# Layer norm with residual: loads of 16 rows instead of 8, and the store queued between the x and the residual load

## The chip, the cores and the metric

One core of a Trainium2 chip. The metric is the device time of one execution in microseconds (us), lower is better. The profile's span is about 1.3 us shorter than that time (237.9 against 239.2 us before).

## The reference

```python
# x, residual: (16, 1024, 512) float32; gamma, beta: (512,)
z = x + residual
mean = np.mean(z, axis=-1, keepdims=True)
var = np.var(z, axis=-1, keepdims=True)
return gamma * (z - mean) / np.sqrt(var + eps) + beta
```

16384 rows of 512 numbers are spread over 128 partitions, 128 rows for each. Below, **"a row" is one row on each of the 128 partitions**: 2 KB per partition, 256 KB in all. So 8 rows are 2 MB and 16 rows 4 MB; x, residual and the result are 128 rows each, 100.67 MB in all.

## The kernel before

The stages: SyncE (SP) issues all large transfers on one queue; GpSimd (POOL) adds the residual to x in place in `zbuf`, 8 rows at a time; ScalarE (ACT) makes the mean and the sum of squares of 4 rows at a time; VectorE (DVE) normalises those 4 rows in place; SP stores them. `zbuf` is a ring of 64 rows, `rbuf` one of 32.

```python
X_CHUNKS = [8] * 15 + [4, 4]          # rows of each load of x
R_CHUNKS = [8] * 15 + [4, 4]          # ... of the residual
OUT_CHUNKS = [16] * 7 + [8, 4, 4]     # rows of each store
Z_ROWS = 64
R_ROWS = 32
STORE_LAG = 40
ADD = 8
# ... cut ...
    stored = 0
    for c, (lo, n) in enumerate(loads_x):             # all on SP, in this order
        asked = lo + n
        while stored < asked - Z_ROWS:                # the ring: x may overwrite
            o = next(i for i, b in enumerate(stores) if b[0] == stored)
            nc.sync.wait_ge(so[o], 16)                # ... only what has been stored
            stored += stores[o][1]
        move(part(zbuf, Z_ROWS, lo, n), dram(xf, lo, n), sx[c])
        while todo_r and todo_r[0][1][0] + todo_r[0][1][1] <= asked:
            rc, (rlo, rn) = todo_r.pop(0)
            wait_rows(s_add, "add", rlo + rn - R_ROWS)
            move(part(rbuf, R_ROWS, rlo, rn), dram(rf, rlo, rn), sr[rc])
        while todo_o and (
            todo_o[0][1][0] + todo_o[0][1][1] <= asked - STORE_LAG or asked == total
        ):
            oc, (olo, on) = todo_o.pop(0)
            wait_rows(s_out, "out", olo + on)         # DVE has written these rows
            move(dram(of, olo, on), part(zbuf, Z_ROWS, olo, on), so[oc])
# ... cut ...
    for c, (lo, n) in enumerate(loads_x):             # POOL
        nc.gpsimd.wait_ge(sx[c], 16)
        for rc, (rlo, rn) in enumerate(loads_r):
            if lo <= rlo < lo + n:
                nc.gpsimd.wait_ge(sr[rc], 16)         # the whole residual load
                for a in range(rlo, rlo + rn, ADD):
                    # zbuf rows a..a+8 += rbuf rows, then s_add += 8
# ... cut: ACT and DVE, loops over 4 rows at a time that wait for s_add and for each other
```

Of the kernel before, what the change touches and what calls it, by code (L numbers as in the profile page):

```python
# [10 lines left out]
ALU = mybir.AluOpType  # L11


X_CHUNKS = [8] * 15 + [4, 4]
R_CHUNKS = [8] * 15 + [4, 4]
OUT_CHUNKS = [16] * 7 + [8, 4, 4]

Z_ROWS = 64
R_ROWS = 32
STORE_LAG = 40  # L20


ADD = 8
# [11 lines left out]
def kernel(  # L35
# [13 lines left out]
    of = out.flatten_outer_dims()  # L49
    N, D = xf.shape  # L50
    inv_d = 1.0 / float(D)
    total = N // P
# [5 lines left out]
    def spans(sizes):  # L58
        assert sum(sizes) == total
        return [(sum(sizes[:c]), n) for c, n in enumerate(sizes)]  # L60

    blocks = spans(OUT_CHUNKS)

    def dram(t, lo, n):

        b0, bn = next(b for b in blocks if b[0] <= lo and lo + n <= b[0] + b[1])
        v = t[P * b0 : P * (b0 + bn), :].rearrange("(p j) d -> p j d", p=P)
        return v[:, lo - b0 : lo - b0 + n, :].rearrange("p a b -> p (a b)")

    zbuf = nc.alloc_sbuf_tensor("zbuf", [P, Z_ROWS * D], FP32)  # L70
# [18 lines left out]
    def sem(name):  # L89
        s = nc.alloc_semaphore(name)  # L90
        sems.append(s)
        return s

    loads_x, loads_r, stores = spans(X_CHUNKS), spans(R_CHUNKS), blocks
    sx = [sem(f"sx{c}") for c in range(len(loads_x))]
# [8 lines left out]
    s_out = sem("out")  # L104
    so = [sem(f"so{c}") for c in range(len(stores))]
# [3 lines left out]
    def part(buf, size, lo, n):  # L109
        assert lo % size + n <= size  # L110
        return buf[:, (lo % size) * D : (lo % size + n) * D]
# [16 lines left out]
    todo_r, todo_o = list(enumerate(loads_r)), list(enumerate(stores))  # L128
# [3 lines left out]
    def wait_rows(s, key, rows):  # L132
        if rows > seen[key]:
            nc.sync.wait_ge(s, rows)
            seen[key] = rows

    def move(out, in_, s):
        i = nc.sync.dma_start(out=out, in_=in_).then_inc(s, 16)  # L138
        if len(first) < EARLY:
            first.append(i.ins)  # L140

    stored = 0
    for c, (lo, n) in enumerate(loads_x):
        asked = lo + n
        while stored < asked - Z_ROWS:
            o = next(i for i, b in enumerate(stores) if b[0] == stored)
            assert all(o != t[0] for t in todo_o)
            nc.sync.wait_ge(so[o], 16)
            stored += stores[o][1]
        move(part(zbuf, Z_ROWS, lo, n), dram(xf, lo, n), sx[c])  # L150
        while todo_r and todo_r[0][1][0] + todo_r[0][1][1] <= asked:
            rc, (rlo, rn) = todo_r.pop(0)
            wait_rows(s_add, "add", rlo + rn - R_ROWS)
            move(part(rbuf, R_ROWS, rlo, rn), dram(rf, rlo, rn), sr[rc])
        while todo_o and (
            todo_o[0][1][0] + todo_o[0][1][1] <= asked - STORE_LAG or asked == total
        ):
            oc, (olo, on) = todo_o.pop(0)
            wait_rows(s_out, "out", olo + on)
            move(dram(of, olo, on), part(zbuf, Z_ROWS, olo, on), so[oc])  # L160



    for o, (lo, n) in enumerate(stores[:-1]):
# [7 lines left out]
    for c, (lo, n) in enumerate(loads_x):  # L172
# [3 lines that stand above are left out]
                assert rlo + rn <= lo + n  # L176
                nc.gpsimd.wait_ge(sr[rc], 16)
                for a in range(rlo, rlo + rn, ADD):
# [3 lines left out]
                        out=z, in0=z, in1=part(rbuf, R_ROWS, a, an), op=ALU.add  # L182
# [9 lines left out]
    with act.Fori(0, total // LAP) as lap:  # L192
        z0 = act.snap((lap * (LAP * D)) % (Z_ROWS * D))
        r0 = act.snap(lap * LAP)
        for j in range(SETS):
# [4 lines left out]
            for k in range(TURN):  # L200
                i = act.activation(  # L201
                    out=junk_m[k][:, :],
# [7 lines left out]
            for k in range(TURN):  # L210
                i = act.activation(  # L211
                    out=junk_s[k][:, :],
# [8 lines left out]
                out=std[j][:, :],  # L221
# [9 lines left out]
    with dve.Fori(0, total // LAP) as lap:  # L231
        z0 = dve.snap((lap * (LAP * D)) % (Z_ROWS * D))
        r0 = dve.snap(lap * LAP)
        for j in range(SETS):
# [3 lines left out]
            for k in range(TURN):  # L238
                dve.scalar_tensor_tensor(  # L239
                    out=zk[k],  # L240
# [9 lines left out]
            for k in range(TURN):  # L250
                i = dve.scalar_tensor_tensor(  # L251
                    out=zk[k],
# [53 lines left out]
```

## Time and profile before

| | before |
|---|---|
| time, median | 239.19 us (239.16 to 239.43, 4 runs) |
| span of the profiled execution | 237.9 us |
| busy share DVE / ACT / POOL | 74% / 78% / 60% |
| share of the 16 DMA engines' span used by the queue | 99.3% |

First, lines of the page: the span; the busy share of the DMA engines in 40 equal slices (9 is 90% or more) and the GB/s of each slice; the row of the queue table (packets, MB, share of the 16 engines' span); and two groups of instructions (busy us, mean ns of one, then the idle time before them and what ended it).

```profile
span 237.9 us, 1484 instructions
...
DMA  8999999999999999999999999999999999999996
GB/s 309 441 433 421 433 433 433 419 427 441 421 438 419 438 427 424 468 441 386 427 433 435 441 413 433 430 449 430 413 430 419 457 441 383 455 435 430 421 417 287
...
q1 hardware_dynamic: 6336, 100.67, 99.3%
...
L181 POOL TENSOR_TENSOR zbuf<-zbuf,rbuf 128x4096 f32<-128x4096 f32 (+1 forms) x17 | 142.0, 8353 | 70.6 <-DMA rbuf<-in_residual_dram 70.6
...
L201 ACT ACTIVATE junk_m<-zbuf 128x512 f32 x128 | 74.8, 585 | 31.5 <-POOL zbuf L181 29.1
```

The queue of transfers is never empty from the first slice to the last, at 423 GB/s over the span. The Trainium skill ("HBM Reference", section Specifications) says that a core streaming alone measures about 425 GB/s; this trace agrees. So POOL's 70.6 us of waiting for the residual and ACT's 29.1 us of waiting for POOL cost nothing: the transfers are the limit.

Adds on POOL in order of time (start us, us, engine, line, operation, then the idle time before it and its releaser):

```profile
149.63 8.87 POOL L181 TENSOR_TENSOR zbuf<-zbuf,rbuf 128x4096 f32<-128x4096 f32 x1 [10.78 <-DMA rbuf<-in_residual_dram]
159.40 8.84 POOL L181 TENSOR_TENSOR zbuf<-zbuf,rbuf 128x4096 f32<-128x4096 f32 x1 [0.90 <-DMA rbuf<-in_residual_dram]
179.00 8.86 POOL L181 TENSOR_TENSOR zbuf<-zbuf,rbuf 128x4096 f32<-128x4096 f32 x1 [10.75 <-DMA rbuf<-in_residual_dram]
188.77 8.85 POOL L181 TENSOR_TENSOR zbuf<-zbuf,rbuf 128x4096 f32<-128x4096 f32 x1 [0.91 <-DMA rbuf<-in_residual_dram]
203.56 4.53 POOL L181 TENSOR_TENSOR zbuf<-zbuf,rbuf 128x2048 f32<-128x2048 f32 x1 [5.94 <-DMA rbuf<-in_residual_dram]
```

Where ACT takes up the rows that are added at 179.00 (rows 104 to 112; 24 rows remain then):

```profile
188.08 0.60 ACT L201 ACTIVATE junk_m<-zbuf 128x512 f32 x1 [5.63 <-POOL zbuf L181]
```

DVE's last piece, same columns:

```profile
226.35 2.72 DVE L251 SCALAR_TENSOR_TENSOR zbuf<-zbuf,rstd,beta_p 128x512 f32 x4
```

And the last 38 us in stretches: start and end, its length, then busy us (and instructions) of PE, PEld, DVE, ACT, POOL, then the granted clock, the DMA share and GB/s. A packet is counted in the stretch in which it starts, so a share can come out a little above 1.

```profile
200.00:210.00 10.00, 0.00 (x0) 0.00 (x0) 9.33 (x17) 9.80 (x30) 6.04 (x2) 1.00 1.04 438
210.00:220.00 10.00, 0.00 (x0) 0.00 (x0) 9.14 (x16) 9.59 (x29) 3.02 (x1) 1.00 1.02 439
220.00:230.00 10.00, 0.00 (x0) 0.00 (x0) 8.78 (x15) 3.63 (x11) 0.00 (x0) 1.00 0.97 415
230.00:238.00 8.00, 0.00 (x0) 0.00 (x0) 0.00 (x0) 0.00 (x0) 0.00 (x0) 1.00 0.75 317
```

DVE is done at 226.35 + 2.72 = 229.07 us, and the span ends at 237.9. Until 230 us the DMA share is at least 0.97: the last stores stand in a queue that is still full, so compute is ahead of the transfers by a few us only.

### The profile page before, as it was taken

The page shows a single profiled execution, that of the slowest core. Times are in us where ns is not written, and L with a number is a line of the kernel's source. Part 1 is how long each engine was busy: PE and PEld are TensorE (multiplying, and loading weights), DVE is VectorE, ACT ScalarE, POOL GpSimd, SP SyncE. Part 2 cuts the span into 40 slices and gives each one's busy share as a digit, 9 for nine tenths or more (in the row PEclk, how much of TensorE's full clock was granted, in tenths as well). Part 3 has the DMA queues.
Part 4 walks back from the last instruction along what each step waited for, and adds up shares of the span by engine and source line. Part 5 has one row for each costly group of instructions (what it writes and reads, how often), then busy time and mean ns, then how long its engine had stood idle before and what let it go on. Part 6 is the DMA issues. An engine that isn't in the chain of part 4 may idle for free.

```text
span 237.9 us, 1484 instructions
## 1 busy us (share of the span) xinstructions
PE 3.7 (2%) x4; PEld 1.2 (0%) x4; DVE 177.2 (74%) x290; ACT 185.5 (78%) x545; POOL 142.2 (60%) x21
## 2 busy tenths in 40 slices
PE   0600000000000000000000000000000000000000
PEld 0100000000000000000000000000000000000000
DVE  0000498989898989898989898963989549898950
ACT  2003999999999999999999999739996399999600
POOL 0098988989889407893078930889209892770000
DMA  8999999999999999999999999999999999999996
GB/s 309 441 433 421 433 433 433 419 427 441 421 438 419 438 427 424 468 441 386 427 433 435 441 413 433 430 449 430 413 430 419 457 441 383 455 435 430 421 417 287
DMA packets 6341, 100.68 MB, mean 423 GB/s; under 512 B 706, under 2 KB 706, under 8 KB 708
## 3 DMA queue, kind: packets, MB, share of 16 engines
q1 hardware_dynamic: 6336, 100.67, 99.3%
q14 instruction: 1, 0.01, 0.0%
q10 hardware_dynamic: 4, 0.00, 0.0%
HBM read 67.11 MB, written 33.55 MB: 423 GB/s over the span
## 4 chain that ended last, share of the span: by engine, by line
DMA 49%; ACT 24%; POOL 11%; DVE 5%; issue 4%; SPq 1%; ACTq 1%; DVEq 0%; POOLq 0%
DMA rbuf<-in_residual_dram 36%; ACT junk_s L211 14%; DMA out_dram<-zbuf 13%; POOL zbuf L181 11%; ACT junk_m L201 10%; DVE zbuf L239 3%; DVE zbuf L251 3%; SPq L138 1%; ACTq L201 1%; DVEq L239 0%; ACT std L220 0%; DVE rstd L248 0%; ACTq L192 0%; ACTq L198 0%; DVEq L231 0%
## 5 line engine op out<-in xcount | busy, mean ns | idle before, releaser
L181 POOL TENSOR_TENSOR zbuf<-zbuf,rbuf 128x4096 f32<-128x4096 f32 (+1 forms) x17 | 142.0, 8353 | 70.6 <-DMA rbuf<-in_residual_dram 70.6
L239 DVE SCALAR_TENSOR_TENSOR zbuf<-zbuf,nm,gamma_p 128x512 f32 x128 | 87.1, 742 | 48.7 <-ACT junk_s L211 48.7
L201 ACT ACTIVATE junk_m<-zbuf 128x512 f32 x128 | 74.8, 585 | 31.5 <-POOL zbuf L181 29.1
L211 ACT ACTIVATE junk_s<-zbuf,nm 128x512 f32 x128 | 88.9, 695 | 1.0
L251 DVE SCALAR_TENSOR_TENSOR zbuf<-zbuf,rstd,beta_p 128x512 f32 x128 | 87.1, 743 | 1.1
L211 ACT ACTIVATION_READ_ACCUMULATOR junk_s<-zbuf,nm 128x1 f32 x128 | 23.9, 187 | 0.0
L201 ACT ACTIVATION_READ_ACCUMULATOR junk_m<-zbuf 128x1 f32 x128 | 23.9, 186 | 0.0
L220 ACT ACTIVATE std<-ssq,eps_t 128x4 f32<-128x4 f32 x32 | 9.5, 297 | 3.0
L248 DVE RECIPROCAL rstd<-std 128x4 f32<-128x4 f32 x32 | 5.4, 170 | 0.0
L189 ACT ACT_TABLE_LOAD x1 | 1.3, 1283 | 2.7 <-PEq L56 2.7
L123 PE MATMUL gamma_p<-gb_row,ones 1*128 1x512 f32 x2 | 2.0, 1118 | 7.2 <-DMA gb_row<-in_gamma_dram 7.2
L123 PE MATMUL beta_p<-gb_row,ones 1*128 1x512 f32 x2 | 1.9, 1052 | 0.0
L118 DVE MEMSET ones<- 1x128 f32 x1 | 0.2, 165 | 2.0 <-PEq L56 2.0
L123 PEld LDWEIGHTS beta_p<-gb_row,ones 1*128 1x128 f32 x2 | 0.7, 328 | 1.0 <-issue 0.5
L123 PEld LDWEIGHTS gamma_p<-gb_row,ones 1*128 1x128 f32 x2 | 0.5, 308 | 7.2 <-issue 7.2
L287 POOL MEMSET const-float32-0.0<- 128x1 f32 x1 | 0.1, 99 | 0.2 <-issue 0.2
L287 POOL MEMSET const-bfloat16-1.0<- 128x1 bf16 x1 | 0.1, 102 | 0.0
L287 POOL MEMSET const-uint8-127<- 128x1 uint8 x1 | 0.1, 102 | 0.0
L287 POOL MEMSET const-float32-1.0<- 128x1 f32 x1 | 0.1, 99 | 0.0
L119 DVE MEMSET eps_t<- 128x1 f32 x1 | 0.1, 59 | 0.0
## 6 DMA issues: line engine op xcount, KB each, us to landing
zbuf<-in_x_dram SPq DMA_DIRECT2D x15, 2048.0 KB, 32.9
rbuf<-in_residual_dram SPq DMA_DIRECT2D x15, 2048.0 KB, 30.1
out_dram<-zbuf SPq DMA_DIRECT2D x7, 4096.0 KB, 28.5
zbuf<-in_x_dram SPq DMA_DIRECT2D x2, 1024.0 KB, 32.5
rbuf<-in_residual_dram SPq DMA_DIRECT2D x2, 1024.0 KB, 34.5
out_dram<-zbuf SPq DMA_DIRECT2D x1, 2048.0 KB, 15.7
out_dram<-zbuf SPq DMA_DIRECT2D x2, 1024.0 KB, 10.4
gb_row<-in_gamma_dram ACTq DMA_DIRECT2D x1, 2.0 KB
```

What stands on the lines that cost most here:

```text
L118: nc.vector.memset(ones[:, :], 1.0).then_inc(s_const, 1)
L123: nc.tensor.matmul(dest[:, :], ones[:, :], gb_row[:, k * D : (k + 1) * D], start=True, stop=True).then_inc(s_pe, 1)
L138: i = nc.sync.dma_start(out=out, in_=in_).then_inc(s, 16)
L181: nc.gpsimd.tensor_tensor(out=z, in0=z, in1=part(rbuf, R_ROWS, a, an), op=ALU.add).then_inc(s_add, an)
L189: act.preload_act_table_set("sqrt_and_others")
L201: i = act.activation(out=junk_m[k][:, :], in_=zk[k], func=ACT.Identity, scale=-inv_d, accum_out=nm[j][:, k : k + 1],)
L211: i = act.activation(out=junk_s[k][:, :], in_=zk[k], func=ACT.Square, bias=nm[j][:, k : k + 1], accum_out=ssq[j][:, k : k + 1],)
L220: act.activation(out=std[j][:, :], in_=ssq[j][:, :], func=ACT.Sqrt, bias=eps_t[:, 0:1], scale=inv_d,).then_inc(s_std, TURN)
L239: dve.scalar_tensor_tensor(out=zk[k], in0=zk[k], scalar=nm[j][:, k : k + 1], in1=gamma_p[:, :], op0=ALU.add, op1=ALU.mult,)
L248: dve.reciprocal(out=rstd[j][:, :], in_=std[j][:, :]).then_inc(s_dve, TURN)
L251: i = dve.scalar_tensor_tensor(out=zk[k], in0=zk[k], scalar=rstd[j][:, k : k + 1], in1=beta_p[:, :], op0=ALU.mult, op1=ALU.add,)
L287: nc = _bacc.Bacc("TRN2", target_bir_lowering=False, num_devices=1)
```

## The change

The intent: fewer, larger loads, and a store that has its turn earlier.

```diff
-X_CHUNKS = [8] * 15 + [4, 4]
-R_CHUNKS = [8] * 15 + [4, 4]
-OUT_CHUNKS = [16] * 7 + [8, 4, 4]
+BLOCK = 16
+TAIL = [8, 4, 4]
+X_CHUNKS = [BLOCK] * 7 + TAIL
+R_CHUNKS = [BLOCK] * 7 + TAIL
+OUT_CHUNKS = [BLOCK] * 7 + TAIL
-STORE_LAG = 40
+STORE_LAG = 48
+    def store_to(rows):
+        while todo_o and todo_o[0][1][0] + todo_o[0][1][1] <= rows:
+            ...                                  # wait for DVE, store: as before
         move(part(zbuf, Z_ROWS, lo, n), dram(xf, lo, n), sx[c])
+        if n == BLOCK:
+            store_to(asked - STORE_LAG)
         while todo_r and todo_r[0][1][0] + todo_r[0][1][1] <= asked:
             ...                                  # the residual load
-        while todo_o and (... <= asked - STORE_LAG or asked == total):
-            ...                                  # the store, behind the residual
+    store_to(total)
```

The same bytes move, the same arithmetic is done, and the adds stay at 8 rows each. In the queue of SP a block of 16 rows was x, residual, x, residual, store; it is now x, store, residual, each of 4 MB. `STORE_LAG` says how many rows further x must have been asked for before a block's store is queued. With loads of 16 rows a lag of 40 would queue each of these stores at the same place as 48, so that line changes nothing by itself.

More of the change, by code (lines that the diff above doesn't have):

```diff
@@ L140, in move @@
             first.append(i.ins)
+    def store_to(rows):
+        while todo_o and todo_o[0][1][0] + todo_o[0][1][1] <= rows:
+            oc, (olo, on) = todo_o.pop(0)
+            wait_rows(s_out, "out", olo + on)
+            move(dram(of, olo, on), part(zbuf, Z_ROWS, olo, on), so[oc])
     stored = 0
@@ L154 @@
             move(part(rbuf, R_ROWS, rlo, rn), dram(rf, rlo, rn), sr[rc])
-        while todo_o and (
-            todo_o[0][1][0] + todo_o[0][1][1] <= asked - STORE_LAG or asked == total
-        ):
-            oc, (olo, on) = todo_o.pop(0)
-            wait_rows(s_out, "out", olo + on)
-            move(dram(of, olo, on), part(zbuf, Z_ROWS, olo, on), so[oc])
+    store_to(total)
     for o, (lo, n) in enumerate(stores[:-1]):
```

## The prediction

> **What bounds it now.** The transfers. The rows of slices give the DMA a busy share of 9 tenths in every slice but the first and last, at about 430 GB/s; the queue table gives the one load/store queue 99.3% of the 16 engines' span. The compute engines have slack (ACT 78%, DVE 74%, POOL 60%), and their waits cost nothing while the queue is full: POOL waits 70.6 us for the residual, ACT 29.1 us for POOL. DVE ends its last row at 229.1 us; the last 1 MB store, queued behind others, still lands before the span ends at 237.9 us: compute stays just ahead of the queue.
>
> **What the change removes.** 30 loads of 16 KB per partition become 14 of 32 KB and a tail. In the trace's packets 16 KB takes 613 ns (median), 32 KB 1213 ns: two small ones cost 13 ns more than a large one; 14 transfers x 8 packets per engine x 13 ns is 1.5 us. The Trainium skill ("DMA: Bandwidth & Descriptors", section Bandwidth) gives 78% of peak at 1 MB and 97% at 16 MB; here the queue is never empty, and the trace leaves only those few ns. By transfers alone the kernel would take about 237.5 us.
>
> **What it adds and moves.** (1) The first add needs both 32 KB pieces: about 21.5 us instead of 12.4. Harmless by itself, the queue being full. (2) A store now stands before a residual load, and six stores (rows 64 to 128) instead of five remain after the last load is asked for. (3) The residual of rows 96 to 112 lands as one block, behind the store of rows 48 to 64: 14 large loads of about 9.75 us, 4 stores of 9.85 us (both from the cadence of landings) and 1.7 us of start give about 178 us. Before, the adds of rows 96 and 104 began at 159.4 and 179.0 us.
>
> **The critical path at the end.** From about 181 us ACT has nothing to do until that block is added: the first 8-row add takes 8.9 us, so ACT resumes near 187.3 us with 32 rows to go, where before it resumed at 188.1 us with 24. ACT takes 11.98 us per 8 rows: the last group of 4 starts near 229 us, DVE has its last row 11.3 us later, at about 240.4. The last store goes into an empty queue: 1.0 us to the first packet, 2.5 us of packets, 0.5 us to the end: span about 244.4 us. The reported time is 1.3 us over the span before, so about 245.5 us. With all loads landed by about 197 us, the last stores wait for DVE, and the DMA idles about 7 us in all between them. A bound of transfers turns into one of compute in the last 65 us: the 1.5 us saved is lost and about 6 more.
>
> **Prediction.** 245.4 us, 8 in 10 between 241.8 and 248.0. Faster by over 2%: 0.02. Within 2%: 0.21. Slower by over 2%: 0.77.
>
> **What the profile would show.** Right: load packets of 32 KB at about 1213 ns; first add at 21 to 22 us; DMA shares full to about 215 us, then with gaps; the chain of waits ending in an unbroken run of ACT from about 187 to 235 us, begun by POOL and the residual; last stores waiting for DVE, whose end is near 240 us. Wrong: a DMA row full to the end, and a span near 236 us.
>
> **What would make it wrong.** Load packets of 32 KB clearly quicker than stores' (the block lands before 175 us), or slower; the residual block landing earlier or later than summed; ACT's pace changing; a store into an empty queue taking more or less than I took from the kernel's start.

## The result, and the profile after

| | before | after |
|---|---|---|
| time, median | 239.19 us (239.16 to 239.43, 4 runs) | 246.16 us (245.74 to 246.48, 4 runs) |
| ratio | | 1.0285 (95% interval 1.027 to 1.030) |
| span of the profiled execution | 237.9 us | 245.1 us |
| queue's share of the 16 engines' span | 99.3% | 96.2% |

A ratio is the mean time of one kernel's fast runs over the mean of the other's fast runs of the same rounds, so not quite the ratio of the medians quoted. The profiled execution of the changed kernel took 246.48 us, the slowest of its four; the lines below are of that one.

The same lines of the page after:

```profile
span 245.1 us, 1463 instructions
...
DMA  8999999999999999999999999999999999969674
GB/s 343 428 428 428 428 433 438 444 444 438 438 358 428 428 428 428 433 433 438 428 428 428 449 444 433 428 428 428 409 425 418 425 456 438 428 283 454 262 299 172
...
q1 hardware_dynamic: 4320, 100.67, 96.2%
...
L185 POOL TENSOR_TENSOR zbuf<-zbuf,rbuf 128x4096 f32<-128x4096 f32 (+1 forms) x17 | 141.6, 8356 | 72.7 <-DMA rbuf<-in_residual_dram 72.7
...
L205 ACT ACTIVATE junk_m<-zbuf 128x512 f32 x128 | 74.9, 585 | 43.7 <-POOL zbuf L185 41.3
```

The queue was busy for 96.2% of 245.1 us = 235.8 us, against 99.3% of 237.9 us = 236.2 us before. So the transfers themselves did not become slower. What is new are gaps, and the row of DMA slices shows where: only in the last five slices (6 9 6 7 4), that is after about 214 us.

The last adds on POOL of the kernel after:

```profile
149.44 17.66 POOL L185 TENSOR_TENSOR zbuf<-zbuf,rbuf 128x4096 f32<-128x4096 f32 x2 [11.51 <-DMA rbuf<-in_residual_dram]
179.17 35.49 POOL L185 TENSOR_TENSOR zbuf<-zbuf,rbuf 128x4096 f32<-128x4096 f32 x5 [12.07 <-DMA rbuf<-in_residual_dram]
```

ACT in the kernel after (same columns):

```profile
188.26 0.60 ACT L205 ACTIVATE junk_m<-zbuf 128x512 f32 x1 [6.01 <-POOL zbuf L185]
```

DVE's last piece in the kernel after:

```profile
238.51 2.72 DVE L255 SCALAR_TENSOR_TENSOR zbuf<-zbuf,rstd,beta_p 128x512 f32 x4
```

`x5` in the add of 179.17 merges five adds that run back to back: two of 8 rows for the block of rows 96 to 112, then those of the tail, which had landed by then. POOL no longer waits at the end; ACT does, before 188.26, for the first of those five.

The chain of work that ended last, in order of time (start us, us, what), where it enters that end:

```profile
140.50 38.51 DMA rbuf<-in_residual_dram
179.17 8.88 POOL zbuf L185
```

The residual load was issued at 140.50 us, directly behind the store of rows 48 to 64, took 38.5 us to land, and released the add with which the end begins.

And the stretches of the end:

```profile
200.00:210.00 10.00, 0.00 (x0) 0.00 (x0) 9.33 (x16) 9.64 (x29) 10.00 (x2) 1.00 1.01 436
210.00:220.00 10.00, 0.00 (x0) 0.00 (x0) 9.14 (x16) 9.59 (x31) 4.66 (x2) 1.00 0.83 357
220.00:230.00 10.00, 0.00 (x0) 0.00 (x0) 9.10 (x16) 9.55 (x29) 0.00 (x0) 1.00 0.73 315
230.00:240.00 10.00, 0.00 (x0) 0.00 (x0) 9.70 (x17) 5.79 (x18) 0.00 (x0) 1.00 0.75 315
240.00:245.00 5.00, 0.00 (x0) 0.00 (x0) 1.23 (x2) 0.00 (x0) 0.00 (x0) 1.00 0.51 210
```

ACT and DVE are busy for over 9 us in each 10 up to 230 us, while the DMA share falls to 0.83, 0.73, 0.75 and 0.51. Before, in the same stretches, ACT's work thinned out from 220 us on, and the DMA share stayed near 1. The limit has changed hands: in the last 57 us (from 188 us) the kernel waits for ACT and DVE, and each of the last stores is issued when DVE ends its rows.

The size of the loss follows from these lines. ACT resumes at the same moment in both kernels (188.08 and 188.26 us), but with 24 rows to go before and 32 after. The 8 rows more put DVE's end from 229.07 to 241.23 us, 12.2 us later. Before, DVE's end had room: the last store, put into an empty queue, would have ended the span about 3.9 us behind it (241.23 to 245.1 in the kernel after), at 233.0 us, and the span ended at 237.9 by the transfers. 12.2 - 4.9 = 7.3 us of the 12.2 show, and the span grew by 7.2.

### The profile page after: what moved, and what is told of

It is laid out like the page before. It is cut to its first block, busy times and chain, and to the rows that moved or that the text cites. A ratio compares the mean times of both kernels' runs of the same rounds, so it can differ in the third digit from the quotient of the medians.

```text
span 245.1 us, 1463 instructions
## 1 busy us (share of the span) xinstructions
PE 4.1 (2%) x4; PEld 1.0 (0%) x4; DVE 177.2 (72%) x290; ACT 185.5 (76%) x545; POOL 141.8 (58%) x21
## 3 DMA queue, kind: packets, MB, share of 16 engines
q1 hardware_dynamic: 4320, 100.67, 96.2%
## 4 chain that ended last, share of the span: by engine, by line
DMA 47%; ACT 33%; POOL 7%; issue 5%; DVE 4%; ACTq 1%; SPq 1%; DVEq 0%; POOLq 0%
DMA rbuf<-in_residual_dram 25%; DMA out_dram<-zbuf 22%; ACT junk_s L215 19%; ACT junk_m L205 14%; POOL zbuf L185 7%; DVE zbuf L243 2%; DVE zbuf L255 2%; ACTq L205 1%; SPq L140 1%; ACT std L224 0%; ACTq L196 0%; DVEq L243 0%; ACTq L202 0%; ACTq L223 0%; DVE rstd L252 0%
```

## The experiments

**The theory ("tail").** With blocks of 16 rows, and a store queued before its residual, the residual of rows 96 to 112 lands at about 179.0 us as one piece. Only then can the last 32 rows pass through POOL (8.9 us for the first add), ACT (about 12 us for each 8 rows) and DVE. That series of compute ends after the transfers would have ended.

**Rivals.** *Sizes*: large loads are slower transfers, or disturb the queue. *Start*: the first add begins at 22.3 us instead of 12.4 us, and all is late by that. *Order*: placing the store before the residual is what costs, whatever the size.

All kernels below gave a correct result. Edits are shown against the changed kernel. The first four ran together on one chip (before: 239.26 us median of 7 runs), the other four on another (before: 239.16 us median of 9).

### residual_halves: the last large residual in two pieces

```diff
-R_CHUNKS = [BLOCK] * 7 + TAIL
+R_CHUNKS = [BLOCK] * 6 + [8, 8] + TAIL
```

> The changed kernel with only the residual of rows 96 to 112 in two transfers of 8 rows. Tail theory (the last large residual lands late and 32 rows of ACT work follow it): the first half lands one 8-row load, 4.9 us, earlier (about 173.8 us), ACT resumes near 183.7 instead of 188.5 us and the time falls to about 241.3 us (ratio to before about 1.009). Rival, large loads are slower everywhere: 13 of 14 are kept, so about 245.7 us. Rival, the late start costs: unchanged, 246.2 us.

Measured: 241.20 us (241.08 to 241.76), ratio 1.0084 (1.0068 to 1.0101). The adds on POOL from the block's first half on:

```profile
173.95 35.50 POOL L185 TENSOR_TENSOR zbuf<-zbuf,rbuf 128x4096 f32<-128x4096 f32 x5 [6.80 <-DMA rbuf<-in_residual_dram]
```

ACT in this run:

```profile
183.05 0.60 ACT L205 ACTIVATE junk_m<-zbuf 128x512 f32 x1 [0.75 <-POOL zbuf L185]
```

The add begins 5.2 us earlier, ACT resumes 5.2 us earlier, and the time is 5.0 us shorter, although 13 of the 14 large loads are untouched. This is one transfer's size changed at one place. *Sizes* and *start* predict no such thing. The Trainium skill ("Perfetto Trace Analysis", section DMA Optimizations) says both that larger transfers use the bandwidth better and that splitting may let some start sooner and may help where the DMA engines are generally idle. In the changed kernel they were not generally idle (96.2% of the span), and the load that was split stood in a full queue; splitting it won 5.0 us all the same, because its first half landed sooner.

### adds_of_4: smaller adds, no transfer changed

```diff
-ADD = 8
+ADD = 4
```

> The changed kernel with the adds on POOL 4 rows at a time instead of 8; no transfer is changed. Tail theory: the residual lands as before at about 178.7 us, the first add of it takes 4.5 instead of 8.9 us, so ACT resumes 4.3 us earlier and the time falls to about 241.8 us (ratio about 1.011). Rival, the transfers themselves are slower: no change, 246.2 us. Rival, the late start: ACT's first row also starts 4.3 us earlier, but it should then have waits in the middle as before; this run alone does not tell it from the tail theory, the run with the first rows halved does.

Measured: 241.39 us (241.36 to 241.50), ratio 1.0089 (1.0072 to 1.0106). The adds on POOL from that block on:

```profile
178.39 35.88 POOL L185 TENSOR_TENSOR zbuf<-zbuf,rbuf 128x2048 f32<-128x2048 f32 x8 [11.17 <-DMA rbuf<-in_residual_dram]
```

ACT in this run:

```profile
183.13 0.60 ACT L205 ACTIVATE junk_m<-zbuf 128x512 f32 x1 [5.39 <-POOL zbuf L185]
```

The add begins nearly as late as in the kernel after (178.39 against 179.17 us), and yet 4.8 us are won: ACT resumes 5.1 us earlier, 0.8 of them by the landing and 4.3 because it gets its first 4 rows after one short add (4.5 us instead of 8.9). So the time between landing and ACT is on the path, and the loss is not in the transfers.

### last_store_behind: one store moved behind its residual

```diff
-        if n == BLOCK:
+        if n == BLOCK and asked < 112:
             store_to(asked - STORE_LAG)
         while todo_r ...                    # the residual load
+        if n == BLOCK and asked >= 112:
+            store_to(asked - STORE_LAG)
```

> The changed kernel with only the store of rows 48 to 64 moved behind the residual of rows 96 to 112 (the other three stay between x and residual). Tail theory: that residual lands one store, 9.8 us, earlier (about 169 us); ACT no longer starves at 181 us but is then limited by what comes next (one short gap of about 1.4 us in the queue near 181 us, where the next x waits for this store); about 240.8 us (ratio about 1.007). Rival, any theory in which the sizes alone cost the time: 246.2 us.

Measured: 242.01 us (241.60 to 242.74), ratio 1.0123 (1.0099 to 1.0146). The last adds on POOL, the block's and those of the tail:

```profile
168.78 17.71 POOL L187 TENSOR_TENSOR zbuf<-zbuf,rbuf 128x4096 f32<-128x4096 f32 x2 [1.77 <-DMA rbuf<-in_residual_dram]
191.03 17.87 POOL L187 TENSOR_TENSOR zbuf<-zbuf,rbuf 128x4096 f32<-128x4096 f32 x3 [4.54 <-DMA rbuf<-in_residual_dram]
```

The residual lands one store earlier (168.78 against 179.17 us), and the time falls by 4.2 us, not by the 5.4 that I expected. The trace's packets show why. The next load of x had to wait for just this store to land, and no packet moved from 177.9 to 179.3 us, the 1.4 us that I expected. But the 16 engines had run out of work one after another before that, which makes 2.2 us of idle time for each on average, and the first packets after the gap were stretched. That load landed 7.65 us after the store, where a load of 8 rows in a full queue takes 4.9. So this one gap cost 2.8 us, not 1.4.

### first_halves: an early start

```diff
-X_CHUNKS = [BLOCK] * 7 + TAIL
-R_CHUNKS = [BLOCK] * 7 + TAIL
+X_CHUNKS = [8, 8] + [BLOCK] * 6 + TAIL
+R_CHUNKS = [8, 8] + [BLOCK] * 6 + TAIL
```

> The changed kernel with only the first 16 rows of x and residual in two pieces each, so that the first add starts near 12.3 us as in the kernel before. Tail theory: no gain, 246.2 us within 0.5 us (ratio about 1.029), ACT resuming at the same 188 us after the last large residual. Rival, the late start of the adds (22.3 instead of 12.4 us) is what costs: about 239 us.

Measured: 245.63 us (245.37 to 246.06), ratio 1.0270 (1.0253 to 1.0288). The first add on POOL, and those from the block on:

```profile
12.43 8.80 POOL L185 TENSOR_TENSOR zbuf<-zbuf,rbuf 128x4096 f32<-128x4096 f32 x1 [11.99 <-DMA rbuf<-in_residual_dram]
...
178.07 35.49 POOL L185 TENSOR_TENSOR zbuf<-zbuf,rbuf 128x4096 f32<-128x4096 f32 x5 [11.58 <-DMA rbuf<-in_residual_dram]
```

The adds begin at 12.43 us as in the kernel before, and nearly nothing is won. *Start* falls. The last block's add begins 1.1 us earlier than in the kernel after, and half a us comes of it.

### store_behind_all: the large loads with the old order

```diff
-        if n == BLOCK:
-            store_to(asked - STORE_LAG)
         while todo_r ...                    # the residual load
+        if n == BLOCK:
+            store_to(asked - STORE_LAG)
```

> The changed kernel with every store issued behind the residual load again, as in the kernel before: the large sizes alone, without the new order. If the new order is what costs: about 238 us. Tail theory with its account of the order: with 64 rows of z and 16-row loads, each of the four x loads from row 64 on must wait for the store queued directly before it, so the queue runs empty four times for 1.5 to 2.1 us each (2.1 us in the run with only the last store behind); the last large residual lands near 175 us, and the time is 244 to 247.5 us, no better than 1.02 of before, with four gaps in the DMA share and SP waiting four times for a store to land just before its x load.

Measured: 251.33 us (251.04 to 251.43), ratio 1.0508 (1.0492 to 1.0524). The direction was right; the size was missed, above the upper end of what I expected. The adds of three blocks:

```profile
113.28 17.70 POOL L185 TENSOR_TENSOR zbuf<-zbuf,rbuf 128x4096 f32<-128x4096 f32 x2 [14.82 <-DMA rbuf<-in_residual_dram]
145.87 17.67 POOL L185 TENSOR_TENSOR zbuf<-zbuf,rbuf 128x4096 f32<-128x4096 f32 x2 [14.89 <-DMA rbuf<-in_residual_dram]
178.46 17.63 POOL L185 TENSOR_TENSOR zbuf<-zbuf,rbuf 128x4096 f32<-128x4096 f32 x2 [14.91 <-DMA rbuf<-in_residual_dram]
```

What SP waited for (us in total, times, longest us):

```profile
SPq L140 <- DMA out_dram<-zbuf: 123.5, 4, 31.3
```

Stretches around the first of the four gaps (columns as before):

```profile
80.00:90.00 10.00, 0.00 (x0) 0.00 (x0) 9.33 (x17) 9.84 (x30) 9.25 (x2) 1.00 0.88 380
90.00:100.00 10.00, 0.00 (x0) 0.00 (x0) 9.10 (x16) 9.55 (x29) 8.46 (x1) 1.00 0.92 367
100.00:112.00 12.00, 0.00 (x0) 0.00 (x0) 11.10 (x19) 11.55 (x35) 0.00 (x0) 1.00 0.99 393
```

The blocks follow each other every 32.6 us (113.28, 145.87, 178.46), where the kernel after takes 29.2 (120.25 to 149.44, the second of them in its lines above). So each of these gaps costs about 3.4 us. The trace's packets and landings divide it: 1.8 us of idle time for each engine on average (1.3 us with no packet at all); about 0.6 us by which the first packets after the gap are stretched, so that the load behind it lands 2.4 us late in all; and 1.0 us more in a second burst of stretched packets, some 20 us after the gap, just ahead of the next store. That burst is why the stretch from 100 to 112 us has a share of 0.99 but only 393 GB/s. What stretches these packets was not tried. The fourth gap, before the small loads of the tail, cost 2.8 us. Four gaps make 13 us.

This is the reason for the new order. `zbuf` holds four blocks of 16 rows, so the x load of a block must wait until the store of the block four earlier has landed. With the store last in the queue, that wait drains the queue. With the residual behind the store, 9.7 us of work remain queued while SP waits. The Trainium skill ("DMA: Bandwidth & Descriptors", section Anatomy of one DMA) explains the form of this, in a section on transfers issued from GpSimd: a wait is served on the issuing sequencer, and the DMA engines just consume their queues; SP's four waits for a store, each before a load of x, show it here. The order, then, bought 5 us of the time against large loads alone (251.3 to 246.2), at the price of the late residual.

### order_only_8: the new order with the small loads

```diff
-X_CHUNKS = [BLOCK] * 7 + TAIL
-R_CHUNKS = [BLOCK] * 7 + TAIL
+X_CHUNKS = [8] * 15 + [4, 4]
+R_CHUNKS = [8] * 15 + [4, 4]
-STORE_LAG = 48
+STORE_LAG = 40
-        if n == BLOCK:
+        if True:
             store_to(asked - STORE_LAG)
```

> The kernel before with only the new order: transfers of 8 rows, lag of 40, but each store queued between the x and the residual load. If the order is harmless by itself: 239.2 us. Tail theory: the residual of 8 rows behind each store lands one store (9.8 us) later, also the last ones; ACT starves before them and ends near 225 us instead of 217 (start of its last group), so about 241.5 to 242.3 us (ratio about 1.012), with 2.5 to 3 us of idle DMA at the end.

Measured: 242.13 us (241.82 to 242.29), ratio 1.0124 (1.0108 to 1.0139). The last adds on POOL:

```profile
178.98 8.85 POOL L185 TENSOR_TENSOR zbuf<-zbuf,rbuf 128x4096 f32<-128x4096 f32 x1 [0.93 <-DMA rbuf<-in_residual_dram]
198.62 17.81 POOL L185 TENSOR_TENSOR zbuf<-zbuf,rbuf 128x4096 f32<-128x4096 f32 x3 [10.79 <-DMA rbuf<-in_residual_dram]
```

The last stretch, up to 240 us (columns as before):

```profile
230.00:240.00 10.00, 0.00 (x0) 0.00 (x0) 6.49 (x11) 1.34 (x5) 0.00 (x0) 1.00 0.60 250
```

Here the residual of rows 112 to 120 stands behind a store, and its add begins at 198.62 us where the kernel before had it at 188.77. The same mechanism at half the block's size costs 3.0 us, with a DMA share of 0.60 in the last 10 us. So *order* is part of the truth, but not a cost of its own: what costs is that the last residuals become late.

### large_then_small and halves_and_adds_of_4: both kernels' good parts

The first keeps 16-row loads for the first 80 rows only; the second joins the two repairs of the tail.

```diff
# large_then_small
-X_CHUNKS = [BLOCK] * 7 + TAIL
-R_CHUNKS = [BLOCK] * 7 + TAIL
+X_CHUNKS = [BLOCK] * 5 + [8] * 4 + TAIL
+R_CHUNKS = [BLOCK] * 5 + [8] * 4 + TAIL
-        if n == BLOCK:
+        if True:
             store_to(asked - STORE_LAG)
# halves_and_adds_of_4
-R_CHUNKS = [BLOCK] * 7 + TAIL
+R_CHUNKS = [BLOCK] * 6 + [8, 8] + TAIL
-ADD = 8
+ADD = 4
```

> The version that the theory points to: 16-row loads for the first 80 rows, 8-row loads for rows 80 to 120, the tail and the order as changed, stores queued also between small loads. Tail theory: ACT's last group starts near 218 us, the queue never runs empty, and what is left is the transfers: 238.2 to 239.2 us (ratio 0.996 to 1.000). If large loads themselves cost something in the first 80 rows: 241 us or more.

> The changed kernel with both repairs of the tail: the residual of rows 96 to 112 in two halves and adds of 4 rows. Each alone left about 3 us of idle DMA at the end (241.2 and 241.4 us). Tail theory: together they bring ACT's last group to about 219 us and the queue stays full to the end: 238 to 239.2 us (ratio 0.995 to 1.000), limited by transfers. A rival in which the two act on the same wait and do not add: about 241 us.

Measured over five rounds: 238.98 us (238.91 to 239.13), ratio 0.9992 (0.9978 to 1.0006); and 239.00 us (238.76 to 239.32), ratio 0.9997 (0.9983 to 1.0010). Lines of the second's page:

```profile
DMA  9999999999999999999999999999999999999997
...
q1 hardware_dynamic: 4464, 100.67, 99.2%
```

Stretches of its end:

```profile
220.00:230.00 10.00, 0.00 (x0) 0.00 (x0) 9.71 (x17) 5.58 (x17) 0.00 (x0) 1.00 0.97 419
230.00:237.00 7.00, 0.00 (x0) 0.00 (x0) 1.03 (x2) 0.00 (x0) 0.00 (x0) 1.00 0.77 325
```

The loss is gone whole, in the second with 13 of the 14 large loads still in place. The two repairs, 5.0 and 4.8 us when alone, add up until the queue is full again (7.2 us), and there they end. *Sizes* falls as an explanation of the loss. But neither version beats the kernel before: the intervals contain 1. The queue's busy time is 99.2% of 237.2 us = 235.3 us, only 0.9 us less than before.

## Why the prediction was right

- **The time**: 245.4 us was predicted, 246.16 us measured, within the range of 241.8 to 248.0, and the class, slower by over 2%, was the one given 0.77.
- **The mechanism**: the add of the late block was to begin at about 178 us and did at 179.17; ACT was to resume near 187.3 us and did at 188.26; DVE's end was to be near 240.4 us and was 238.51 + 2.72 = 241.2; the last store's way through an empty queue, 4.0 us by my sum, took 245.1 - 241.2 = 3.9 us. That it is the late block and the compute behind it is shown from three sides: landing it earlier by size (residual_halves) or by place (last_store_behind) and shortening the add behind it (adds_of_4) each win 4.2 to 5.0 us, and two together win all 7.2.
- **The late start is harmless**: shown by first_halves.
- **The saving in transfers was mis-sized**: from packets of 613 and 1213 ns I took 1.5 us off; the queue's busy time fell by 0.4 us (236.2 to 235.8). The 32 KB load packets did take 1213 ns in the median, as predicted, but some took more: at about 67 to 70 us some 30 of them were stretched by 0.1 to 1.1 us. Spread over the 16 engines this burst is 0.9 us of the 1.1 us that are missing. The load of x for rows 48 to 64, the last before the first store, so landed 10.3 us after the load before it, where its neighbours took 9.7. The six kernels that begin with 16-row loads and keep the store ahead of its residual all show it, at 10.1 to 10.4 us. What stretches these packets was not tried and stays open.
- **The landing was mis-sized by more than the total shows**: 1.7 us of start, 14 loads of 9.75 us and 4 stores of 9.85 us make 177.6 us, and the block landed at 179.0. The first load landed at 12.4 us where this sum has 11.45; the loads of x for rows 48 to 64 and 96 to 112 were 1.2 us over together; the other transfers were 0.8 us under. The load of rows 96 to 112, 10.4 us here, took 9.7 us in residual_halves, adds_of_4, last_store_behind and first_halves, so that part seems to belong to this execution. From ACT's start to DVE's end the prediction had 53.1 us and the trace has 53.0, so by these sums the excess over the prediction, 0.8 us in the time, came with the late landing.
- **The size of a gap** was wrong in two expectations of the experiments, not in the prediction: I took 1.4 to 2.1 us for a queue that runs empty, and 2.8 to 3.4 us were measured.

## What to carry to other kernels

A kernel bound by its transfers can lose time through a change that leaves the transfers as fast as they were: ask when the last inputs land, in what piece, and how much compute must still follow, and compare that end with the end of the queue. Here large blocks were free early in the stream and one cost time at its end, and it was as good to cut the compute step behind the landing (4.8 us won) as the transfer (5.0 us). When a ring of buffers makes a load wait for a store, keep one other transfer queued behind that store, and look at what this makes late.

## What the Trainium skill lacked or had wrong

- "DMA: Bandwidth & Descriptors", section Bandwidth, gives efficiencies of single transfers (78% at 1 MB, 97% at 16 MB) and a rule to batch. They were measured on transfers issued from GpSimd; here SP issues them. The section lacks a comparison of sizes for transfers that stand one behind another in a queue, where here the size from 2 MB up hardly mattered: the kernel before, with loads of 2 MB, kept its queue busy 99.3% of the span at 423 GB/s, and 14 loads of 4 MB took 0.4 us of 236 off.
- The same page, section Anatomy of one DMA, puts the fixed cost of a transfer at about 2 us (measured there on transfers issued from GpSimd). It lacks what an emptied queue costs: 2.8 us in last_store_behind and 2.8 to 3.4 us for each of four in store_behind_all, of which 1.8 to 2.2 us were idle time of the engines and the rest lay in stretched packets after the gap.
- "Perfetto Trace Analysis", section DMA Optimizations, advises larger transfers, above all for those under 2 KB and in kernels bound by DMA, and splitting where the DMA engines are generally idle. It lacks the place in the stream, which decided in these runs, with the engines busy 96.2% of the span: 16-row loads were free for the first 80 rows (ratio 0.9992) and cost 5 us in one residual at the end (246.16 against 241.20 us).
